# Second norm of an encoder trunk: the second half of the tokens prepared 384 columns at a time, squares on ScalarE summed in a tree

## The chip, the cores and the metric

One core of one Trainium2 chip runs the whole program. The metric is device time in microseconds (us), the median of several runs; lower is better. The engines are named as in the profile: PE (matrix multiplies), DVE (VectorE), ACT (ScalarE), POOL (GpSimd), SP (issues the DMAs).

## The reference

Two layers act on 512 prompt tokens and 256 sample tokens (768 columns here), model width 1024. All is float32.

```
for l in range(DEPTH):                                  # 2
    h = rms_norm(x, norm_mix[l])
    proj = h @ w_in[l]                                  # q, k, v of three mixers
    ...                                                 # global, neighbourhood and dilated attention
    x = x + y @ w_out[l]
    h = rms_norm(x, norm_ffn[l])                        # the part that changes
    gate, up = jnp.split(h @ w_gate_up[l], 2, axis=-1)
    x = x + (jax.nn.silu(gate) * up) @ w_down[l]
```

## The kernel before

**Layout.** Features lie on the 128 partitions (8 chunks `k` of 128), tokens on the columns, and `X` holds the residual. The tokens are three groups `p` of 256; the last norm of a layer takes them in the order 2, 0, 1. For the FFN they are two halves of 384 columns. Every operand of a float32 product is split into a high part (rounded to the matmul's type) and a low part (the rest), and one product is three matmuls (`mm3`, L544: high-high, high-low, low-high).

**Who sets the order.** Each operation is recorded with a priority, a set of engines that it may run on, and a cost. `Plan.emit` simulates the engines with these costs and fixes on which engine, in which buffers and in which order everything is issued. On the chip each engine then runs its list strictly in order, and SP its DMA list too. A cost therefore changes orders and choices, never the work itself, and one changed cost can reorder everything behind it.

**`norm2` (L632)** runs between the attention's output projection (`emit_out`; its last step, L1026, adds into `X`) and the FFN.
- `parts` (L643) makes a high part on ACT (L646) and a low part on DVE (L649, or L652 where a gain is applied as well).
- `half1` splits the first half's columns: operands A and B.
- `half2` does the second half's: C, D and the four sums T1 to T4, built from E1 (L679), T2 (L681), T3 (L684) and T4 (L687). Their scratch buffers lie in the tiles `ppa` (D) and `p`, `bt` (E1, T2, T3, T4). It is called twice, for columns 0 to 128 once groups 2 and 0 are ready, for 128 to 384 once group 1 is.
- `squares` (L586) then squares the group's `X`: 4 squares (L591 on DVE, L592 on ACT), each added (L594) into one of two buffers of the tile `tbm`, folded (L707), split (L560, L561), summed over partitions by two matmuls (`root`, L566), and turned by ACT's Ln and Exp (L569, L571) into `row`, the 1/rms of each token. Since there is one such pair of buffers, the groups take turns.

**`emit_ffn` (L1077)** computes the first two blocks of 128 FFN features (f = 0, 1) as plain products: 192 matmuls of 384 columns in 8 PSUM banks, with weights prepared by `plain` (L1033; low part L1037). DVE multiplies each bank by `row` (L1099), ACT applies SiLU (L1082, after a table load), POOL multiplies gate and up (L1083), and SP writes the result to DRAM (`spill`, L1084). The other 20 blocks use seven products (`PRODUCTS`, L1062) in place of eight, on summed weights (`sums`, L1041: DMA loads L1049, sums L1053, high parts L1056, low parts L1057) and on A, B, D, T1 to T4. The first product of a block is A11 with A.

Of the kernel before, what the change touches and what calls it, by code (L numbers as in the profile page):

```python
# [10 lines left out]
AF = mybir.ActivationFunctionType  # L11
# [35 lines left out]
     nsq='ACT', nadd='DVE', nhi='ACT DVE', nlo='POOL', yhl='DVE POOL', tout=0, tdn=1, n1=2, nf=86, sf=5, om=1,  # L47
     nsq0='ACT DVE', nadd0='DVE POOL', nhi0='ACT DVE', nlo0='POOL,DVE', nsq2='ACT,DVE', nadd2='DVE,POOL', nhi2='ACT',
     nlo2='DVE POOL', qs=0.0, nsp=0.0, nsp2=0.0, w0i=(0, 0, 1, 1), w0d='DVE,POOL', w0p=-19.5, l2=(0, 1), lo=0, vhi='ACT',
# [31 lines left out]
class Plan:  # L81
# [3 lines left out]
    HOP = 0.15  # L85
    FIFO = {"S", "P", "PT", "PTS", "PO", "OT", "OV", "Y", "TB", "BT", "GP", "GS", "W", "RAW", "ACT", "SG", "SQ", "YR", "YT", "RB", "MC", "CS", "QKG", "WG", "WF", "WU", "U", "UL", "UG", "UC", "ROW", "R0", "R1", "RX", "NR", "ND1", "ND2", "H", "H1"}
    GROUP = {"MC": "TB", "WG": "W", "WF": "W", "WU": "W", "UL": "U", "UG": "U", "R0": "RAW", "R1": "RAW", "RX": "RAW", "H1": "H"}
    PSUM = {"D", "S", "PT", "PO", "M", "ANY", "LB"}
# [218 lines left out]
def trunk(ctx: ExitStack, tc: tile.TileContext, t):  # L307
# [324 lines left out]
    def norm2(l, bs):  # L632
# [26 lines left out]

        def half2(ps, a, z, pr):  # L660

            n = z - a
            x = lambda half, kk: X[:, kk, half * HALF + a:half * HALF + z]
            rx = lambda k: [("x", p, kk // 2) for p in ps for kk in (k, k + 4)] + ["gcol"]
            Ds = [P.buf("ND1" if n == 128 else "ND2") for k in range(4)]
            v = lambda b: b[0][:, :n]
            for k in range(4):
                u, D = U[k], Ds[k]
                g0, g1 = gcol[:, l, 2, k:k + 1], gcol[:, l, 2, k + 4:k + 5]
                parts(lambda k=k: x(1, k), u["C"], a, z, g0, rx(k), pr)  # L670
                dve(n, lambda D=D, k=k, g1=g1: DVE.tensor_scalar(v(D), x(1, k + 4), g1, None, op0=OP.mult), r=rx(k), w=[D],
                    prio=pr, fast=True, lock=True, ptr=True)
                parts(lambda D=D: v(D), u["D"], a, z, None, [D], pr)
            pr = L + 198.2
            for k in range(4):
                u, D = U[k], Ds[k]
                g0, g1 = gcol[:, l, 2, k:k + 1], gcol[:, l, 2, k + 4:k + 5]
                E1, T2, T3, T4 = (P.buf("NR") for _ in range(4))
                ew(n, lambda E, E1=E1, k=k: E.tensor_tensor(v(E1), x(1, k), x(0, k), op=OP.subtract), r=rx(k), w=[E1], prio=pr,  # L679
                   on="DVE POOL")  # L680
                dve(n, lambda T2=T2, E1=E1, D=D, g0=g0: DVE.scalar_tensor_tensor(  # L681
                    v(T2), v(E1), g0, v(D), op0=OP.mult, op1=OP.subtract), r=[D, E1, "gcol"], w=[T2], prio=pr, lock=True, ptr=True)
# [45 lines left out]
    def emit_qkv(l, g, bs, wp, gains, rope):  # L728
# [6 lines left out]
        for p in order(g):  # L735
# [91 lines left out]
    def emit_attn(l, g, gs, bs, mc):  # L827
# [15 lines left out]
        for p in order(g):  # L843
# [467 lines left out]
```

## Time and profile before

| what | value |
|---|---|
| median of 3 runs | 1782.69 us (1782.56 to 1784.72) |
| the profiled execution's own time | 1784.08 us |
| its span, first to last instruction | 1782.3 us |
| mean granted PE clock | 0.989 |
| busy: PE, DVE, ACT, POOL | 1712.3, 1310.0, 917.7, 542.0 us |

A busy share is an average over stages with different limits. What matters here is where PE stands still, and what the trace names as the end of the wait (in brackets behind a row of the timeline: idle us, then the releaser). Matmuls are pipelined: the time from one start to the next is a matmul's price, not its duration.

### The profile page before, as it was taken

How to read it: one execution, taken by the hardware profiler on the slowest of the kernel's cores; microseconds unless marked ns; L12 is line 12 of the kernel's file. 1: busy time of each engine (PE TensorE's matmuls, PEld its weight loads, DVE VectorE, ACT ScalarE, POOL GpSimd, SP SyncE). 2: the span in 40 equal slices, each digit the busy share in tenths (PEclk: the TensorE clock that was granted, in tenths of full speed). 3: DMA queues.
4: the chain of work that ended last, by engine and by line, in shares of the span. 5: the costliest groups of instructions: out<-in, count | busy, mean ns of one | idle time of the engine just before them, and what ended most of it. 6: DMA issues, size and time to landing. Idle time of an engine off the chain costs nothing.

```text
span 1782.3 us, 30961 instructions
## 1 busy us (share of the span) xinstructions
PE 1712.3 (96%) x11504; PEld 1682.5 (94%) x11504; DVE 1310.0 (74%) x2511; ACT 917.7 (51%) x2151; POOL 542.0 (30%) x577
## 2 busy tenths in 40 slices
PE   5999999897999999999999999998979999999999
PEld 5999999797999999999999999997979999999999
DVE  7788678699988887543668886777998888864433
ACT  5887577565444444321358775866644444442220
POOL 1565144223233333100015543642223333320000
PEclk9999999998999999999999999999989999999999
DMA  5321111102333332533222201111133333343332
GB/s 158 81 63 49 36 34 51 36 19 91 112 106 103 102 104 90 153 122 104 72 62 62 75 25 36 47 33 36 33 117 100 101 105 104 103 118 123 116 110 72
DMA packets 96200, 145.29 MB, mean 82 GB/s; under 512 B 28720, under 2 KB 58416, under 8 KB 96048
## 3 DMA queue, kind: packets, MB, share of 16 engines
q1 hardware_dynamic: 96048, 143.31, 26.7%
q8 instruction: 90, 1.47, 0.4%
q14 instruction: 62, 0.51, 0.1%
HBM read 122.82 MB, written 20.45 MB: 80 GB/s over the span
## 4 chain that ended last, share of the span: by engine, by line
PE 81%; DVE 10%; ACT 7%; issue 1%; DMA 1%; SPq 0%; DVEq 0%
PE ps L546 24%; PE ps L547 24%; PE ps L548 24%; PE ps L956 3%; PE ps L934 2%; PE ps L875 2%; ACT p L922 1%; ACT u L941 1%; DVE u L652 1%; ACT w L521 1%; DVE w L522 1%; PE ps L807 1%; DVE u L649 1%; DVE x L1026 1%; DVE u L942 1%
## 5 line engine op out<-in xcount | busy, mean ns | idle before, releaser
L548 PE MATMUL ps<-u,w 128*128 128x384 f32 (+1 forms) x1684 | 559.7, 332 | 9.7 <-DVE w L1057 9.7
L546 PE MATMUL ps<-u,w 128*128 128x384 f32 (+1 forms) x1684 | 559.8, 332 | 5.4 <-ACT w L1056 4.6
L547 PE MATMUL ps<-u,w 128*128 128x384 f32 (+1 forms) x1684 | 559.3, 332 | 0.0
L548 PEld LDWEIGHTS ps<-u,w 128*128 128x128 f32 x1684 | 317.8, 189 | 10.6 <-DVE w L1057 10.6
L546 PEld LDWEIGHTS ps<-u,w 128*128 128x128 f32 x1684 | 317.7, 189 | 6.5 <-ACT w L1056 4.9
L547 PEld LDWEIGHTS ps<-u,w 128*128 128x128 f32 x1684 | 317.8, 189 | 0.0
L546 PE MATMUL ps<-w,u 128*128 128x256 f32 x768 | 228.8, 298 | 12.5 <-ACT w L521 9.3
L547 PE MATMUL ps<-w,u 128*128 128x256 f32 x768 | 219.1, 285 | 5.3 <-DVE w L522 5.3
L548 PE MATMUL ps<-w,u 128*128 128x256 f32 x768 | 219.2, 285 | 0.0
L521 ACT CAST w<-raw 128x1024 fp32r<-128x1024 f32 (+2 forms) x102 | 94.9, 932 | 209.2 <-PE ps L547 187.8
L1159 DVE TENSOR_TENSOR x<-x,ps 128x384 f32<-128x384 f32 x96 | 51.4, 553 | 154.4 <-PE ps L548 154.4
L546 PEld LDWEIGHTS ps<-w,u 128*128 128x128 f32 x768 | 148.6, 193 | 14.6 <-ACT w L521 9.3
L547 PEld LDWEIGHTS ps<-w,u 128*128 128x128 f32 x768 | 148.9, 194 | 6.3 <-DVE w L522 5.6
L548 PEld LDWEIGHTS ps<-w,u 128*128 128x128 f32 x768 | 148.5, 193 | 0.0
L546 PE MATMUL ps<-yt,w 128*128 128x256 f32 x392 | 114.3, 291 | 3.9 <-DVE x L1026 3.8
L522 DVE TENSOR_TENSOR w<-raw,w 128x768 fp32r<-128x768 f32 (+2 forms) x87 | 97.2, 1119 | 24.8 <-ACT w L521 17.8
L956 PE MATMUL ps<-u 128*128 128x256 f32 (+1 forms) x592 | 105.6, 296 | 9.4 <-DVE u L942 4.6
L547 PE MATMUL ps<-yt,w 128*128 128x256 f32 x392 | 111.9, 286 | 0.2 <-DVE yt L1012 0.2
L548 PE MATMUL ps<-yt,w 128*128 128x256 f32 x392 | 111.6, 285 | 0.0
L942 DVE TENSOR_TENSOR u<-ps,u 128x512 fp32r<-128x512 f32 (+1 forms) x160 | 97.2, 625 | 18.2 <-ACT u L941 17.4
L875 PE MATMUL ps<-u 128*128 128x256 f32 (+1 forms) x384 | 94.8, 349 | 7.8 <-DVE sm L919 3.9
L956 PEld LDWEIGHTS ps<-u 128*128 128x128 f32 x592 | 84.7, 194 | 14.6 <-DVE u L942 7.1
(253 smaller groups left out, 3711.8 us busy)
## 6 DMA issues: line engine op xcount, KB each, us to landing
raw<-in_w_down SPq DMA_DIRECT2D x48, 384.0 KB, 3.2
raw<-in_w_gu SPq DMA_DIRECT2D x68, 256.0 KB, 3.0
spill<-y SPq DMA_DIRECT2D x86, 192.0 KB, 3.0
raw<-in_w_in SPq DMA_DIRECT2D x32, 512.0 KB, 3.6
p<-in_w_gu SPq DMA_DIRECT2D x51, 256.0 KB, 3.3
ppa<-in_w_gu SPq DMA_DIRECT2D x35, 256.0 KB, 3.2
raw<-in_w_out SPq DMA_DIRECT2D x16, 512.0 KB, 3.6
tbm<-in_w_gu SPq DMA_DIRECT2D x22, 256.0 KB, 2.9
```

The lines of the kernel that those rows point to most:

```text
L521: act(n, lambda hs=hs: ACT.copy(self.flat(0)[:, hs], raw[0][:, hs]), r=[raw], w=[(b, 0) + z], prio=prio)
L522: ew(n, lambda E, hs=hs: E.tensor_tensor(self.flat(1)[:, hs], raw[0][:, hs], self.flat(0)[:, hs].bitcast(F32), op=OP.subtract), r=[raw, (b ...
L546: PE.matmul(out, a[0], b[0], start=start, stop=False, skip_group_check=on)
L547: PE.matmul(out, a[0], b[1], start=False, stop=False, skip_group_check=on)
L548: PE.matmul(out, a[1], b[0], start=False, stop=stop, skip_group_check=on)
L649: ew(n, lambda E: E.tensor_tensor(lo(b, a, z), src(), hi(b, a, z).bitcast(F32), op=OP.subtract), r=r + [(b, 0, a)], w=[(b, 1, a)], prio=pr ...
L652: dve(n, lambda: DVE.scalar_tensor_tensor(lo(b, a, z), src(), g, hi(b, a, z).bitcast(F32), op0=OP.mult, op1=OP.subtract), r=r + [(b, 0, a) ...
L875: PE.matmul(S[0][:, :nk], q, kk[:, k0:k0 + nk], start=i == 0, stop=i == 1)
L934: PE.transpose(pt[0][:, i * 128:(i + 1) * 128], PP[j][0][:, c * 128:(c + 1) * 128], ident)
L942: dve(n, lambda n=n, pt=pt, ps_=ps_: DVE.tensor_tensor(ps_[1][:, :n], pt[0][:, :n], ps_[0][:, :n].bitcast(F32), op=OP.subtract), r=[pt, (p ...
L956: PE.matmul(po[0][:, o:o + wd], v, ps_[i][:, z * wd:(z + 1) * wd], start=first and z == 0 and i == 0, stop=end and (last or more), **({} i ...
L1159: dve(HALF, lambda xv=xv, acc=accs[h]: DVE.tensor_tensor(xv(), xv(), acc[0][:, :HALF], op=OP.add), r=[accs[h]], w=[("x", p, c // 2) for p ...
```

## The change

- `half2` runs once, for all 384 columns of the second half, when group 1 is ready. D's product may run on ACT too (`ndd`).
- The squares of a group go to four buffers of the tile `p` (`HS`), all on ACT (before: ACT and DVE by turns); the adds form a tree and all run on DVE (before, in layer 0, DVE and POOL by turns).
- The squares and the root get a priority of 0.3 behind the group's splits; the sums T1 to T4 keep 198.2. The scratch of E1, T2, T3, T4 is now 5 buffers in `p` and one in `bt`, so that most of it is free only when the last squares are used up.
- The planner's costs for copies of 64 partitions are raised: `kcp1`, `kcp2` (L822) and L966 from 256 to 400 columns, the add L971 from 256 to 336.

```diff
-     nsq0='ACT DVE', nadd0='DVE POOL', nhi0='ACT DVE', nlo0='POOL,DVE', nsq2='ACT,DVE', nadd2='DVE,POOL', nhi2='ACT',
+     nsq0='ACT DVE', nadd0='DVE POOL', nhi0='ACT DVE', nlo0='POOL,DVE', nsq2='ACT', ndd='DVE ACT', nadd2='DVE', nhi2='ACT',
...
-    P.storage("ND1", [(a,) for a in cut(ppa, "ppa", 4, 128)])
-    P.storage("ND2", [(a,) for a in cut(ppa, "ppa", 4, 256, 512)])
-    P.storage("NR", [(a,) for a in cut(pt_, "p", 8, 256) + cut(btr, "bt", 2, 256)])
+    P.storage("ND", [(a,) for a in cut(ppa, "ppa", 4, HALF)])
+    P.storage("NR", [(a,) for a in cut(pt_, "p", 5, HALF) + cut(btr, "bt", 1, HALF)])
...
-    P.storage("H", [tbh])
+    P.storage("HS", [tuple(ptile)])
...
-                dve(n, lambda D=D, k=k, g1=g1: DVE.tensor_scalar(v(D), x(1, k + 4), g1, None, op0=OP.mult), r=rx(k), w=[D],
-                    prio=pr, fast=True, lock=True, ptr=True)
+                ew(n, lambda E, D=D, k=k, g1=g1: E.tensor_scalar(v(D), x(1, k + 4), g1, None, op0=OP.mult), r=rx(k), w=[D],
+                   prio=pr, fast=True, ptr=True, extra=1, on="ndd",
+                   act=lambda D=D, k=k, g1=g1: ACT.activation(v(D), x(1, k + 4), AF.Copy, scale=g1))
...
-            pr, h = bs[p], P.buf("H")
+            pr, h = bs[p], P.buf("HS")
             if p == 2:
                 half1(2, 0, 256, pr)
             elif p == 0:
                 half1(0, 256, HALF, pr)
-                half2((2, 0), 0, 128, pr)
             else:
-                half2((2, 0, 1), 128, HALF, pr)
-            pr += K["nsp2"]
-            squares(p, h, "2", pr)
+                half2((2, 0, 1), pr)
+            pr += 0.3
+            for c in range(4):
+                xc = lambda p=p, c=c: xT(p)[:, 2 * c:2 * c + 2]
+                v = lambda h=h, c=c: h[c].rearrange("p (k t) -> p k t", k=2)
+                ew(512, lambda E, v=v, xc=xc: E.tensor_tensor(v(), xc(), xc(), op=OP.mult), r=[("x", p, c)], w=[(h, c)],
+                   prio=pr, on="nsq2", act=lambda v=v, xc=xc: ACT.activation(v(), xc(), AF.Square))
+            for i, j in ((0, 1), (2, 3), (0, 2)):
+                ew(512, lambda E, h=h, i=i, j=j: E.tensor_tensor(h[i], h[i], h[j], op=OP.add), r=[(h, j)], w=[(h, i)], prio=pr,
+                   on="nadd2")
...
-                ew(256, lambda E, dst=dst, sp=sp: E.tensor_copy(dst(), sp()), r=[pk], w=[(gs[p], "k", p, i)], prio=pr,
+                ew(400 if i else 256, lambda E, dst=dst, sp=sp: E.tensor_copy(dst(), sp()), r=[pk], w=[(gs[p], "k", p, i)], prio=pr,
```

In the changed file the lines behind `norm2` stand 6 further down (L1049 is L1055, L1057 is L1063), those of `mm3`, `root` and `parts` one further up (L566 is L565), and T2, T3, T4 keep theirs. The tree's adds are L707 there, the fold is L713.

DVE in layer 0 at the last group's root, before: the fifth of the eight banks' multiplies (L1099), the root's low part (L561), the other multiplies, then the first sums (L1053) and low parts (L1057) of block f = 2's weights.

```order
L1099 TENSOR_TENSOR y<-ps_77,row 128x384
L561 TENSOR_TENSOR yt<-tbm,yt 128x256
L1099 TENSOR_TENSOR sq<-ps_75,row 128x384
L1099 TENSOR_TENSOR sq<-ps_71,row 128x384
L1099 TENSOR_TENSOR y<-ps_72,row 128x384
L1099 TENSOR_TENSOR y<-ps_74,row 128x384
L1053 TENSOR_TENSOR ppa<-raw 128x512
L1057 TENSOR_TENSOR w<-raw,w 128x512
```

The same root in the changed program: its tree (L707), fold (L713) and low part (L560), among bank multiplies (L1105) and plain weights' low parts (L1043), and behind it the first T2, T3, T4 (L681, L684, L687).

```order
L707 TENSOR_TENSOR p<-p 128x512
L1105 TENSOR_TENSOR y<-ps_73,row 128x384
L707 TENSOR_TENSOR p<-p 128x512
L1043 TENSOR_TENSOR w<-raw,w 128x512
L707 TENSOR_TENSOR p<-p 128x512
L1043 TENSOR_TENSOR w<-raw,w 128x512
L713 TENSOR_TENSOR p<-p 128x256
L1105 TENSOR_TENSOR y<-ps_74,row 128x384
L1105 TENSOR_TENSOR y<-ps_75,row 128x384
L560 TENSOR_TENSOR yt<-p,yt 128x256
L681 SCALAR_TENSOR_TENSOR p<-bt,gcol,ppa 128x384
L684 SCALAR_TENSOR_TENSOR p<-x,gcol,ppa 128x384
```

Some 30 rows further on, still DVE of the changed program, the end of the sums: the last chunk's low parts (L648, L651), the last two bank multiplies, then the first weight sum (L1059) and the low part of A11 (L1063, out of `tbm`).

```order
L648 TENSOR_TENSOR u<-bt,u 128x384
L648 TENSOR_TENSOR u<-p,u 128x384
L651 SCALAR_TENSOR_TENSOR u<-p,gcol,u 128x384
L1105 TENSOR_TENSOR y<-ps_72,row 128x384
L1105 TENSOR_TENSOR y<-ps_73,row 128x384
L1059 TENSOR_TENSOR raw<-tbm 128x512
L1063 TENSOR_TENSOR w<-tbm,w 128x512
```

What moved: before, the last root stood behind all sums and just ahead of the weights; now it stands ahead of all sums, and the low part of the first weight behind all of them. Layer 1 has the same rows in the changed program.

SP in layer 0, before, from the eight loads of the plain weights (L1035) on: three loads of block f = 2 (L1049), a spill (L1084), the fourth load.

```order
L1035 DMA raw<-in_w_gu 128x512 x8
L1049 DMA raw<-in_w_gu 128x512 x3
L1084 DMA spill<-y 128x384
L1049 DMA raw<-in_w_gu 128x512
L1084 DMA spill<-y 128x384
```

SP at the same place in the changed program (L1041, L1055, L1090).

```order
L1041 DMA raw<-in_w_gu 128x512 x8
L1055 DMA tbm<-in_w_gu 128x512 x2
L1055 DMA raw<-in_w_gu 128x512 x2
L1090 DMA spill<-y 128x384 x2
L1090 DMA spill<-sq 128x384
```

All four loads now stand ahead of the first spill, two of them in `tbm`, which the squares no longer use.

## Rows read from the trace of the kernel before

**Rows 1.** The page: PE's busy time and share.

```profile
PE 1712.3 (96%) x11504; PEld 1682.5 (94%) x11504; DVE 1310.0 (74%) x2511; ACT 917.7 (51%) x2151; POOL 542.0 (30%) x577
```

**Rows 2.** Who PE waited for, whole span: total us, times, longest.

```profile
PE ps L548 <- DVE w L1057: 9.7, 2, 9.4
```

**Rows 3.** Busy us of each engine (instructions) in stretches; PEclk, DMA share, GB/s.

```profile
40.00:382.00 342.00, 328.70 (x2628) 316.13 (x2627) 261.51 (x613) 241.69 (x655) 153.05 (x195) 1.00 0.16 46
410.50:420.50 10.00, 1.56 (x5) 0.65 (x3) 7.35 (x18) 6.86 (x14) 1.76 (x3) 0.63 0.00 0
420.50:427.00 6.50, 6.11 (x18) 5.60 (x19) 6.34 (x7) 2.69 (x6) 3.61 (x3) 0.51 0.66 214
433.00:860.00 427.00, 427.00 (x2464) 426.79 (x2463) 300.63 (x454) 162.68 (x298) 104.64 (x82) 1.00 0.36 108
860.00:1262.00 402.00, 386.54 (x3077) 372.94 (x3076) 307.75 (x696) 268.75 (x711) 155.57 (x195) 0.99 0.17 47
1293.00:1303.00 10.00, 0.62 (x4) 0.30 (x3) 10.00 (x24) 3.81 (x10) 1.10 (x1) 0.71 0.41 135
1303.00:1307.50 4.50, 4.50 (x14) 4.50 (x15) 4.46 (x8) 3.84 (x7) 0.00 (x0) 0.50 0.40 121
```

**Rows 4.** Timeline of PE, layer 0: start, us, instruction, [idle before <-releaser].

```profile
410.56 0.34 PE L548 MATMUL ps<-u,w 128*128 128x384 f32 x1
413.90 0.58 PE L566 MATMUL ps<-yt,ones 128*128 128x256 f32 x1 [3.00 <-ACT yt L560]
...
420.54 0.69 PE L546 MATMUL ps<-u,w 128*128 128x384 f32 x1 [4.59 <-ACT w L1056]
...
421.90 0.69 PE L548 MATMUL ps<-u,w 128*128 128x384 f32 x1 [0.36 <-DVE w L1057]
```

**Rows 5.** Timeline of PE, layer 1.

```profile
1293.17 0.34 PE L547 MATMUL ps<-u,w 128*128 128x384 f32 x1
1302.89 0.69 PE L548 MATMUL ps<-u,w 128*128 128x384 f32 x1 [9.38 <-DVE w L1057]
```

**Rows 6.** Timeline of DVE, layer 0.

```profile
363.82 2.45 DVE L652 SCALAR_TENSOR_TENSOR u<-x,gcol,u 128x256 fp32r<-128x256 f32 x6
...
368.60 1.12 DVE L652 SCALAR_TENSOR_TENSOR u<-x,gcol,u 128x128 fp32r<-128x128 f32 x4
...
380.67 1.27 DVE L1026 TENSOR_TENSOR x<-ps,x 128x512 f32<-128x512 f32 x2
...
384.17 0.34 DVE L671 TENSOR_SCALAR ppa<-x,gcol 128x256 f32<-128x256 f32 x1
...
388.25 1.88 DVE L1037 TENSOR_TENSOR w<-raw,w 128x512 fp32r<-128x512 f32 x3
...
405.83 1.47 DVE L1099 TENSOR_TENSOR y<-ps,row 128x384 f32<-128x384 f32 x3
```

**Rows 7.** Timeline of DVE, layer 1.

```profile
1261.49 0.68 DVE L1026 TENSOR_TENSOR x<-ps,x 128x512 f32<-128x512 f32 x1
...
1285.61 1.51 DVE L652 SCALAR_TENSOR_TENSOR u<-p,gcol,u 128x256 fp32r<-128x256 f32 x1
...
1302.16 0.68 DVE L1057 TENSOR_TENSOR w<-raw,w 128x512 fp32r<-128x512 f32 x1
```

**Rows 8.** Timeline of POOL, layer 1.

```profile
1285.34 1.50 POOL L1057 TENSOR_TENSOR w<-raw,w 128x512 fp32r<-128x512 f32 x1 [5.32 <-ACT w L1056]
```

**Rows 9.** Timeline of ACT, layer 0.

```profile
381.29 1.30 ACT L646 ACTIVATE u<-x,gcol 128x256 fp32r<-128x256 f32 x3
...
402.64 0.63 ACT L592 ACTIVATE tbm<-x 128x512 f32<-128x512 f32 x1
...
416.92 1.28 ACT L1082 ACT_TABLE_LOAD   x1
```

**Rows 10.** Groups by line and form: busy us, mean ns of one, idle before.

```profile
L971 DVE TENSOR_TENSOR y<-ps,y 64x256 f32<-64x256 f32 x96 | 39.9, 415 | 12.0 <-ACT y L966 9.6 <-issue 0.3
L822 ACT CAST u<-ps 64x256 fp32r<-64x256 f32 x96 | 35.2, 367 | 10.9 <-DVE u L821 7.4 <-PE ps L811 2.2
```

More of the change, by code (lines that the diff above doesn't have):

```diff
@@ L56 @@
      nadd='DVE POOL', nhi='ACT DVE', nlo='POOL', yhl='DVE POOL', tout=0, tdn=1, n1=2, nf=86, sf=5, om=1,
-     nsq0='ACT', nadd0='DVE POOL', nhi0='ACT', nlo0='POOL', nsq2='ACT,DVE', nadd2='DVE', nhi2='ACT', nlo2='DVE POOL', qs=0.0,
+     nsq0='ACT', nadd0='DVE POOL', nhi0='ACT', nlo0='POOL', nsq2='ACT', ndd='DVE ACT', nadd2='DVE', nhi2='ACT', nlo2='DVE POOL', qs=0.0,
      nsp=0.0, nsp2=0.0, w0i=(0, 1, 2, 2), w0d='DVE,POOL', w0p=-19.5, l2=(0, 1), lo=0, vhi='ACT', vlo='DVE POOL', gu2='POOL',
@@ L85 @@
     HOP = 0.15
-    FIFO = {"S", "P", "PT", "PTS", "PO", "OT", "OV", "Y", "TB", "BT", "GP", "GS", "W", "RAW", "ACT", "SG", "SQ", "YR", "YT", "RB", "MC", "CS", "QKG", "WG", "WF", "WU", "U", "UL", "UG", "UC", "ROW", "R0", "R1", "RX", "NR", "ND1", "ND2", "H", "H1"}
-    GROUP = {"MC": "TB", "WG": "W", "WF": "W", "WU": "W", "UL": "U", "UG": "U", "R0": "RAW", "R1": "RAW", "RX": "RAW", "H1": "H"}
+    FIFO = {"S", "P", "PT", "PTS", "PO", "OT", "OV", "Y", "TB", "BT", "GP", "GS", "W", "RAW", "ACT", "SG", "SQ", "YR", "YT", "RB", "MC", "CS", "QKG", "WG", "WF", "WU", "U", "UL", "UG", "UC", "ROW", "R0", "R1", "RX", "NR", "ND", "HS", "H", "H1"}
+    GROUP = {"MC": "TB", "WG": "W", "WF": "W", "WU": "W", "UL": "U", "UG": "U", "R0": "RAW", "R1": "RAW", "RX": "RAW", "H1": "H", "HS": "H"}
     PSUM = {"D", "S", "PT", "PO", "M", "ANY", "LB"}
@@ L658, in half1, with half2 @@
                 parts(lambda k=k: X[:, k, a:z], b, a, z, gcol[:, l, 2, k:k + 1], [("x", p, k // 2), "gcol"], pr)
-        def half2(ps, a, z, pr):
-            n = z - a
-            x = lambda half, kk: X[:, kk, half * HALF + a:half * HALF + z]
+        def half2(ps, pr):
+            n = HALF
+            x = lambda half, kk: X[:, kk, half * HALF:half * HALF + HALF]
             rx = lambda k: [("x", p, kk // 2) for p in ps for kk in (k, k + 4)] + ["gcol"]
-            Ds = [P.buf("ND1" if n == 128 else "ND2") for k in range(4)]
+            Ds = [P.buf("ND") for k in range(4)]
             v = lambda b: b[0][:, :n]
@@ L669, in half2 @@
                 g0, g1 = gcol[:, l, 2, k:k + 1], gcol[:, l, 2, k + 4:k + 5]
-                parts(lambda k=k: x(1, k), u["C"], a, z, g0, rx(k), pr)
-                dve(n, lambda D=D, k=k, g1=g1: DVE.tensor_scalar(v(D), x(1, k + 4), g1, None, op0=OP.mult), r=rx(k), w=[D],
-                    prio=pr, fast=True, lock=True, ptr=True)
-                parts(lambda D=D: v(D), u["D"], a, z, None, [D], pr)
+                parts(lambda k=k: x(1, k), u["C"], 0, n, g0, rx(k), pr)
+                ew(n, lambda E, D=D, k=k, g1=g1: E.tensor_scalar(v(D), x(1, k + 4), g1, None, op0=OP.mult), r=rx(k), w=[D],
+                   prio=pr, fast=True, ptr=True, extra=1, on="ndd",
+                   act=lambda D=D, k=k, g1=g1: ACT.activation(v(D), x(1, k + 4), AF.Copy, scale=g1))
+                parts(lambda D=D: v(D), u["D"], 0, n, None, [D], pr)
             pr = L + 198.2
@@ L682, in half2 @@
                     v(T2), v(E1), g0, v(D), op0=OP.mult, op1=OP.subtract), r=[D, E1, "gcol"], w=[T2], prio=pr, lock=True, ptr=True)
-                parts(lambda T2=T2: v(T2), u["T2"], a, z, None, [T2], pr)
+                parts(lambda T2=T2: v(T2), u["T2"], 0, n, None, [T2], pr)
                 dve(n, lambda T3=T3, D=D, k=k, g0=g0: DVE.scalar_tensor_tensor(
                     v(T3), x(1, k), g0, v(D), op0=OP.mult, op1=OP.subtract), r=rx(k) + [D], w=[T3], prio=pr, lock=True, ptr=True)
-                parts(lambda T3=T3: v(T3), u["T3"], a, z, None, [T3], pr)
+                parts(lambda T3=T3: v(T3), u["T3"], 0, n, None, [T3], pr)
                 dve(n, lambda T4=T4, T2=T2, k=k, g1=g1: DVE.scalar_tensor_tensor(
                     v(T4), x(0, k + 4), g1, v(T2), op0=OP.mult, op1=OP.add), r=rx(k) + [T2], w=[T4], prio=pr, lock=True, ptr=True)
-                parts(lambda T4=T4: v(T4), u["T4"], a, z, None, [T4], pr)
-                parts(lambda E1=E1: v(E1), u["T1"], a, z, g0, [E1, "gcol"], pr)
+                parts(lambda T4=T4: v(T4), u["T4"], 0, n, None, [T4], pr)
+                parts(lambda E1=E1: v(E1), u["T1"], 0, n, g0, [E1, "gcol"], pr)
         for p in order(NG - 1):
-            pr, h = bs[p], P.buf("H")
+            pr, h = bs[p], P.buf("HS")
             if p == 2:
@@ L965, in emit_attn @@
                 ts = slice(h * 256, h * 256 + 256)
-                act(256, lambda yr=yr, po=po, hs=hs, ts=ts: ACT.copy(yr[0][hs, :], po[0][64:128, ts]), r=[po], w=[(yr, h)],
+                act(400, lambda yr=yr, po=po, hs=hs, ts=ts: ACT.copy(yr[0][hs, :], po[0][64:128, ts]), r=[po], w=[(yr, h)],
                     prio=pr, sbuf=False)
@@ L970, in emit_attn @@
                 ts = slice(h * 256, h * 256 + 256)
-                dve(256, lambda yr=yr, po=po, hs=hs, ts=ts: DVE.tensor_tensor(
+                dve(336, lambda yr=yr, po=po, hs=hs, ts=ts: DVE.tensor_tensor(
                     yr[0][hs, :], po[0][0:64, ts], yr[0][hs, :], op=OP.add), r=[po], w=[(yr, h)], prio=pr)
```

## The prediction

> **What bounds the kernel now.** I read the page first: PE is busy for 96% of the span [rows 1]. That says little, since matmuls overlap: one of 384 columns lasts 0.34 us [rows 4], but in the FFN's long stretch 2464 of them take 427.0 us, 0.173 us each, with no idle time and clock 1.00 [rows 3]. Nothing is to be had there, so I went on to the other stretches of that table. PE is bare at two places, 410.5 to 420.5 (1.56 us busy) and 1293 to 1303 (0.62 us) [rows 3], the end of `norm2` in each layer. The two attention stretches, 342 and 402 us, leave PE idle for 13.3 and 15.5 us, 28.8 together [rows 3].
>
> The list of waits names DVE's low part of a weight (L1057) as the longest [rows 2], and the timelines tell what is late. Layer 0: the 192 plain products are issued by 410.56, the last root waits for its split until 413.90, and the first matmul of block f = 2 starts at 420.54 only, behind ACT's high part, which is queued behind the table load and the SiLUs that need the root (the load stands at 416.92 [rows 9]). Its third matmul, which needs the weight's low part, starts at 421.90 [rows 4]. Layer 1: PE stops after the second matmul of that block at 1293.17 and goes on at 1302.89, when DVE has done the low part at 1302.16 [rows 5, 7]; DVE is busy for all 10.00 us between [rows 3]. So from the last add into `X` (end 381.94 in layer 0, 1262.17 in layer 1 [rows 6, 7]) to that low part DVE needs 40.0 and 40.7 us, and PE has only about 29 to 31 us of other work. Behind each wait the clock is at its lower level, 1.2 of 2.4 GHz: 0.51 and 0.50 of full speed for 6.5 and 4.5 us [rows 3].
>
> **The change part by part.** I price DVE's new list from the last add into `X`, time T, to A11's low part. The order gives the counts.
>
> Prices. L652 on 256 columns: six in 2.45, 0.41 each; on 128: four in 1.12, 0.28 each [rows 6]; the step of 0.13 gives an estimated 0.54 at 384. A two-tensor operation on 384 columns: L1099, three in 1.47, 0.49. On 512: L1037, three in 1.88, 0.63. D's product: 0.34 at 256 columns [rows 6]; I keep 0.34, since the step to 384 matters little for three of them.
>
> *Up to the root.* 3 D products (1.0), 4 low parts of C (2.2), 4 of D (2.0), 4 low parts of plain weights and 3 tree adds (7 x 0.63 = 4.4), 3 bank multiplies (1.5), fold and root's low part (0.8): 11.8. ACT in that time has 4 C parts, 4 D casts, one D product, Ln and Exp, 4 squares and 3 weight casts; with 0.43 for a scaled part of 256 columns and 0.63 for a square [rows 9], 0.5 a piece elsewhere and 0.6 for a weight cast, that is about 10. It is close behind DVE, so DVE will wait for a square once or twice: I add 1.0 (0 to 2).
>
> *The sums.* 16 operations at 0.54 (8.6), 12 low parts, 3 E1 and 5 bank multiplies at 0.49 (9.8), one weight sum and the low part itself (1.3): 19.7. As a check from the other side: merging the widths saves 0.41 + 0.28 - 0.54 = 0.15 on each of the 20 scaled operations, 3.0 a layer, and six squares that leave DVE save 6 x 0.63 = 3.8; 6.8 in all, which is what layer 1 gains by the sum (40.7 - 34.0). In layer 0 six adds come back from POOL, three of 512 columns and three of 256, at most 3 us; with them go POOL's delays.
>
> *POOL beside DVE.* In layer 1 an L652 that usually takes 0.41 took 1.51: it began at 1285.61 while POOL ran from 1285.34 to 1286.84 [rows 7, 8]. In the new order POOL has four gate products (L1089) behind its first E1, some beside the sums: 0 to 4 such delays of 1.1, 0 to 4.4. I take 1.5, since most of the gate products wait for late bank multiplies.
>
> Sum: 11.8 + 1.0 + 19.7 + 1.5 = **34.0 us**, against 40.0 and 40.7. T itself moves: 30 plain matmuls stand ahead of the last output projection where 24 stood, 6 x 0.173 = 1.0 later. The third matmul of block 2 then starts near 381.94 + 1.0 + 34.0 = 416.9 in layer 0, 5.0 ahead of 421.90, and near 1297.2 in layer 1, 5.7 ahead of 1302.89. PE still stops, for 4 to 6 us a layer, so I keep the stretch at the low clock as it is.
>
> What else must be in time: the four weight loads now stand ahead of the spills and two go to `tbm`, so data and ACT's cast are there before DVE. The sums cannot start before the last root (their scratch lies in `p`), which costs nothing if DVE has other work; until then it has the 11.8 us. T2 is needed 24 matmuls (4.2 us) behind A11's start, and it is complete before A11's low part. The steps behind (S1, S2 and their low parts, 5 x 0.63 = 3.2) fit under those 24 matmuls. Squares and D's product on ACT cost PE nothing while ACT stays under DVE's 34 us.
>
> The raised costs: a copy of 64 x 256 takes 0.367 on ACT, the add 0.415 on DVE [rows 10]; the planner's cost functions gave 0.265 and 0.337 for them (0.052 + 256/1200 and 0.07 + 256/960) and now give 0.385 and 0.42. They add no work, yet the attention of both layers is dealt anew. No row says what the new order costs; the bounds are the 28.8 us that PE idles there now, less or more. I take 0, since the new costs lie nearer the rows, and plus or minus 4 for the likeliest case.
>
> Total: 5.0 + 5.7 = 10.7. The profiled execution took 1784.08 (span 1782.3 and 1.8 around it): 1773.4. The median of the runs lies 1.4 below it, so I forecast **1772 us**. A measurement tells about 0.2% (3.6 us) from no change: faster is below 1779.1, slower above 1786.3.
>
> **The rivals.**
> - *The wait only moves* (1781). If every gate product on POOL holds DVE for its whole length, not one operation in three, the four take 4 x 1.5 = 6.0 in place of 1.5 [rows 8]: the chain is 38.5, the gain 10.7 - 9.0 = 1.7, near 1781. For it: A11's low part, which the list of waits blames, now stands behind all sums. Against it: 24 DVE instructions fit into the 10.00 us of layer 1's wait, with POOL busy for 1.10 of them [rows 3], so most of the sums have POOL's side free.
>  The Trainium skill, "SBUF — State Buffer", section "SBUF: two separate sides", says that a VectorE operation with two SBUF inputs and a GpSimd operation that reads SBUF exclude each other for a whole instruction. By that rule this rival would be the forecast; the 1.51 us agree with it for one instruction, and no row here shows it for all kinds.
> - *The wait vanishes* (1760). If DVE and ACT stay ahead, PE runs through: the third matmul follows two others (0.35 us) on 410.73 in layer 0, 10.8 us earlier, and 0.17 us on 1293.17 in layer 1, 9.5 earlier; the half-speed stretches give back up to half of 6.5 and 4.5 us, of which I count 3. That is 23.3 in all, 1784.1 - 23.3 - 1.4 = 1759.4. Against it: the sum would have to be wrong by 6 us a layer.
> - *Slower: the new order of the attention* (1787 and up). PE loses there what norm2 gains as soon as its 28.8 us of idle time grow by 10.7, and it is measurably slower from 14.3 on, half as much again. For it: every queue is in-order and the order differs from early in layer 0. Against it: the planner's new costs are the measured ones within 5%, and PE there is 96% busy whatever the order has been.
>
> **How the numbers follow.** Forecast (1766 to 1778): 0.60. Wait moves: 0.13. Wait vanishes: 0.12. Attention: 0.15. Faster 0.60 + 0.12 = 0.72, same 0.13, slower 0.15. The range 1762 to 1784 takes in the moved wait and half of the vanished one; about 0.06 lies below it and 0.13 above.
>
> **What would show it.** Right: in both layers PE's last root (L565) stands amid the plain products with a wait under 1.5 us; PE then stops once, for 4 to 6 us, on DVE's L1063; from the last add into `X` to the end of that low part there are 34 us, of them some 13 to the root's split. The load of the fourth weight is issued ahead of any spill. Wrong: a wait of PE at that place for ACT or a DMA, DVE idle among the sums for want of scratch buffers or casts (a chain near 40), or idle time of PE in the attention stretches that differs from 13.3 and 15.5 us by more than 4.

## The result, and the profile after

| | median | runs |
|---|---|---|
| before | 1782.67 us | 1782.56 to 1784.72 |
| changed | 1761.39 us | 1760.31 to 1764.65 |

The ratio is 0.9881 (95% interval 0.9864 to 0.9898): 21.3 us faster. The forecast was 1772 us, 10.7 faster, in a range of 1762 to 1784. The direction was right; the gain was twice as large, and the time fell 0.6 us below the range.

The page of the changed kernel, its row of busy times (answers to [rows 1]), and from the list of PE's waits the entry that answers to [rows 2]:

```profile
PE 1703.2 (97%) x11504; PEld 1678.5 (95%) x11504; DVE 1295.1 (74%) x2430; ACT 917.0 (52%) x2117; POOL 532.7 (30%) x556
```

```profile
PE ps L547 <- DVE w L1063: 8.2, 2, 4.1
```

The number of matmuls is the same; DVE has 81 instructions fewer. The wait for A11's low part is now PE's only one at this place, 4.1 us in each layer. PE's timeline at it, layer 0 and layer 1 (answers to [rows 4, 5]):

```profile
390.39 0.40 PE L565 MATMUL ps<-yt,ones 128*128 128x256 f32 x2
...
406.40 0.34 PE L546 MATMUL ps<-u,w 128*128 128x384 f32 x1
410.83 0.44 PE L547 MATMUL ps<-u,w 128*128 128x384 f32 x1 [4.10 <-DVE w L1063]
...
1272.45 0.34 PE L546 MATMUL ps<-u,w 128*128 128x384 f32 x1
1276.91 0.69 PE L547 MATMUL ps<-u,w 128*128 128x384 f32 x1 [4.12 <-DVE w L1063]
```

The last root (first row) is now summed amid the plain products, without a wait; before it came 23.5 us later, after a wait of 3.00 [rows 4]. DVE's timeline, layer 0 and then layer 1 (answers to [rows 6, 7]), shows the last add into `X`, the root's low part, and A11's low part:

```profile
377.92 0.68 DVE L1032 TENSOR_TENSOR x<-ps,x 128x512 f32<-128x512 f32 x1
...
389.44 0.42 DVE L560 TENSOR_TENSOR yt<-p,yt 128x256 fp32r<-128x256 f32 x1
...
410.10 0.68 DVE L1063 TENSOR_TENSOR w<-tbm,w 128x512 fp32r<-128x512 f32 x1
...
1243.98 0.69 DVE L1032 TENSOR_TENSOR x<-ps,x 128x512 f32<-128x512 f32 x1
...
1276.17 0.69 DVE L1063 TENSOR_TENSOR w<-tbm,w 128x512 fp32r<-128x512 f32 x1
```

From the end of the last add (378.60, 1244.67) to that of the low part (410.78, 1276.86) DVE needs 32.2 us in both layers, where it needed 39.9 and 40.7 (the prediction's 40.0 runs to PE's start at 421.90 [rows 4]). And the last add itself comes earlier: 3.3 us in layer 0 (381.94 before).

The table of stretches (answers to [rows 3]). The second attention stretch begins at the same distance ahead of the FFN's last add as 860 did before:

```profile
40.00:378.60 338.60, 325.91 (x2638) 315.68 (x2637) 260.72 (x603) 243.50 (x654) 150.52 (x190) 1.00 0.17 48
406.50:410.50 4.00, 0.24 (x2) 0.00 (x0) 4.00 (x9) 1.79 (x4) 0.75 (x1) 1.00 0.85 278
410.50:416.00 5.50, 5.17 (x20) 5.17 (x21) 5.47 (x9) 2.56 (x5) 2.96 (x1) 0.69 0.33 93
847.00:1244.70 397.70, 385.42 (x3086) 373.30 (x3085) 307.74 (x689) 270.27 (x708) 151.87 (x186) 1.00 0.17 49
1272.00:1277.00 5.00, 0.88 (x6) 0.56 (x4) 5.00 (x11) 2.07 (x4) 1.17 (x1) 0.79 0.71 231
1277.00:1284.00 7.00, 7.00 (x28) 7.00 (x29) 6.66 (x10) 4.06 (x8) 2.53 (x1) 0.66 0.41 132
```

The two attention stretches take 338.6 + 397.7 = 736.3 us in place of 342 + 402 = 744 [rows 3]. That is a third of the whole gain, in a part of the kernel to which the change adds no work and from which it takes none. (Six more plain matmuls even stand ahead of the last output projection now, 30 where 24 stood.) While PE waits, DVE is busy for all 4.00 and 5.00 us: the end of `norm2` is still DVE's. The granted clock behind the wait is 0.69 and 0.66, part of the stretch at the lower of its two levels, 1.2 GHz.

In terms of the span: 1782.3 - 1758.5 = 23.8 us, of which 7.9 is the earlier last add (3.3 in layer 0, 4.6 in layer 1, counted from layer 0's last FFN add on), 16.2 the shorter chains from the last add to A11's low part (7.7 and 8.5), and -0.3 what follows (1.9 gained in layer 0, 2.2 lost in layer 1).

### The profile page after: what moved, and what is told of

It reads as the page before. It is cut to its first block, busy times and chain, and to the rows that moved or that the text cites. A ratio compares the mean times of both kernels' runs of the same rounds, so it can differ in the third digit from the quotient of the medians.

```text
span 1758.5 us, 30838 instructions
## 1 busy us (share of the span) xinstructions
PE 1703.2 (97%) x11504; PEld 1678.5 (95%) x11504; DVE 1295.1 (74%) x2430; ACT 917.0 (52%) x2117; POOL 532.7 (30%) x556
## 5 line engine op out<-in xcount | busy, mean ns | idle before, releaser
L962 PE MATMUL ps<-u 128*128 128x256 f32 (+1 forms) x592 | 102.2, 292 | 6.0 <-DVE y L977 3.6
L521 DVE TENSOR_TENSOR w<-raw,w 128x768 fp32r<-128x768 f32 (+2 forms) x84 | 88.9, 1060 | 17.5 <-ACT w L520 12.0
L881 PE MATMUL ps<-u 128*128 128x256 f32 (+1 forms) x384 | 93.4, 350 | 5.0 <-DVE sm L925 2.7
L962 PEld LDWEIGHTS ps<-u 128*128 128x128 f32 x592 | 82.7, 191 | 10.7 <-DVE y L977 4.6
```

What stands on the lines that cost most here:

```text
L521: ew(n, lambda E, hs=hs: E.tensor_tensor(self.flat(1)[:, hs], raw[0][:, hs], self.flat(0)[:, hs].bitcast(F32), op=OP.subtract), r=[raw, (b ...
L881: PE.matmul(S[0][:, :nk], q, kk[:, k0:k0 + nk], start=i == 0, stop=i == 1)
L962: PE.matmul(po[0][:, o:o + wd], v, ps_[i][:, z * wd:(z + 1) * wd], start=first and z == 0 and i == 0, stop=end and (last or more), **({} i ...
```

## The experiments

Each time stands beside runs of the kernel before on the same chip, whose medians were 1782.5 (E1 to E4), 1783.5 (E5 to E8), 1783.2 (E9 to E12), 1782.7 (E13 to E16) and 1782.6 us (E17, E18). The theory after the result: the planner's three numbers dealt attention anew and gave the part that the forecast took as zero. The rival: the new norm itself frees the attention's tail.

### E1 and E2: the two parts of the change apart

E1 is the kernel before with the three numbers; E2 is the changed kernel without them.

```diff
-                ew(256, lambda E, dst=dst, sp=sp: E.tensor_copy(dst(), sp()), r=[pk], w=[(gs[p], "k", p, i)], prio=pr,
+                ew(400 if i else 256, lambda E, dst=dst, sp=sp: E.tensor_copy(dst(), sp()), r=[pk], w=[(gs[p], "k", p, i)], prio=pr,
...
-                act(256, lambda yr=yr, po=po, hs=hs, ts=ts: ACT.copy(yr[0][hs, :], po[0][64:128, ts]), r=[po], w=[(yr, h)],
+                act(400, lambda yr=yr, po=po, hs=hs, ts=ts: ACT.copy(yr[0][hs, :], po[0][64:128, ts]), r=[po], w=[(yr, h)],
...
-                dve(256, lambda yr=yr, po=po, hs=hs, ts=ts: DVE.tensor_tensor(
+                dve(336, lambda yr=yr, po=po, hs=hs, ts=ts: DVE.tensor_tensor(
```

> The kernel before with nothing changed but the three numbers that the planner is given for the last two key copies (400 for 256), the copy of the attention product's second half (400) and the addition of the out-projection's inputs (336); second half of the tokens, its sums and its squares stay as they were. Theory A (the new order of attention is where the unforeseen gain comes from): about 8 to 10 us faster, some 1773 us, with the last addition into X at about 379 to 380 us in layer 0 (381.94 before). Rival B (the attention's tail is freed by the rewritten norm, and the numbers are worth nothing): within 3 us of 1782.7, last addition still at about 382 us.

> The changed kernel with the three numbers put back to 256, so that only the norm before the feed-forward part is changed. Theory A: what the forecast took for that part, 11 to 16 us, so 1767 to 1772 us, with the last addition into X at 381.9 to 383 us in layer 0. Rival B: nothing is lost by putting the numbers back, 1760 to 1763 us, last addition at about 379 us.

E1: 1774.44 us, ratio 0.9958 (0.9946 to 0.9971), 8.1 us faster. E2: 1768.47, ratio 0.9921 (0.9909 to 0.9934), 14.0 faster. Their sum is 22.1, the change's gain 21.3. The attention stretches of E1 and then of E2, and between them the last adds of E1 and E2 in layer 0:

```profile
40.00:377.80 337.80, 325.09 (x2634) 314.86 (x2633) 261.04 (x608) 241.29 (x654) 153.95 (x195) 1.00 0.17 47
857.30:1253.20 395.90, 382.33 (x3076) 370.24 (x3075) 307.72 (x696) 267.38 (x707) 153.13 (x189) 1.00 0.17 48
```

```profile
376.36 1.41 DVE L1026 TENSOR_TENSOR x<-ps,x 128x512 f32<-128x512 f32 x2
```

```profile
380.54 1.28 DVE L1032 TENSOR_TENSOR x<-ps,x 128x512 f32<-128x512 f32 x2
```

```profile
40.00:381.90 341.90, 328.61 (x2628) 316.02 (x2627) 259.13 (x602) 243.21 (x653) 149.79 (x190) 1.00 0.17 48
851.30:1252.70 401.40, 386.03 (x3080) 372.12 (x3079) 306.48 (x683) 270.18 (x708) 154.04 (x192) 1.00 0.17 48
```

With the numbers the two stretches sum to 733.7 us, without them to 743.3, nearly the 744 of before. The rival falls: the new norm leaves the attention as long as it was.

The numbers do not act on the attention alone. In E1, with the old norm, the chain from the last add to A11's low part takes 41.5 and 41.6 us where it took 39.9 and 40.7, so part of the 10.3 us by which the stretches shrank is lost again. In E2, with the new norm in the old order, the chain is 34.6 and 34.5 us, some 2.4 longer than in the change (last adds until 381.82 and 1252.69). E2's low parts of A11 in layer 0 and layer 1:

```profile
415.71 0.68 DVE L1063 TENSOR_TENSOR yt<-raw,yt 128x512 fp32r<-128x512 f32 x1
...
1286.53 0.68 DVE L1063 TENSOR_TENSOR yt<-raw,yt 128x512 fp32r<-128x512 f32 x1
```

### E3 and E5: wide sums or new squares alone

Both have the three numbers. E3 is the changed kernel with the squares of before:

```diff
-    P.storage("HS", [tuple(ptile)])
+    P.storage("HS", [tbh])
...
-            pr += 0.3
-            for c in range(4):
...
-            for i, j in ((0, 1), (2, 3), (0, 2)):
...
+            squares(p, h, "2", pr)
```

> The changed kernel with the three new numbers and the sums formed 384 columns wide, but the squares of the second norm as before (two tiles of 256 columns for each part, dealt to ScalarE and VectorE, added by VectorE or GpSimd, not held back). My working of the forecast put about half of the chain's gain on the way from the last addition to the root (14.5 us before, 11.8 after) and the other half on the sums. Theory A: 3 to 8 us slower than the changed kernel, 1764 to 1769 us. Rival: the squares cost nothing on this way because the root is not what PE waits for, 1760 to 1763 us.

E5 is the other half: E1 with the squares and adds of the change, and `half2` still called twice, for 128 and 256 columns.

```diff
-            pr += K["nsp2"]
-            squares(p, h, "2", pr)
+            pr += 0.3
+            for c in range(4):
...
+            for i, j in ((0, 1), (2, 3), (0, 2)):
...
```

> The kernel before with the three numbers for the planner (400, 400, 336) and with the new squares alone: all on ScalarE, added in a tree on VectorE in the four tiles of p, 0.3 behind the parts; the second half of the tokens and its sums stay in two pieces of 128 and 256 columns. E3 was the other half of it, the merged sums without the new squares, and gained nothing over E1 (1774.07 against 1774.44). Theory R (the root ahead of the sums carries the gain; merging saves DVE at most 3.0 us a layer): 1761 to 1768 us, with the last root's split on DVE about 12 us behind the last addition into X. Rival (neither half is worth anything alone, as DVE's list only becomes short enough with both): 1771 to 1775 us.

E3: 1774.07 us, ratio 0.9956 (0.9944 to 0.9969). E5: 1773.95, ratio 0.9942 (0.993 to 0.9955). Against E1's 1774.44 either half alone gives nothing that can be told from noise (the intervals of E1, E3 and E5 overlap), and both together give 13 us. Both expectations that I favoured were missed. In E3, PE and ACT in layer 0:

```profile
410.94 0.39 PE L565 MATMUL ps<-yt,ones 128*128 128x256 f32 x1 [1.02 <-ACT yt L559]
...
416.61 0.69 PE L545 MATMUL ps<-u,w 128*128 128x384 f32 x1 [4.59 <-ACT w L1054]
```

```profile
412.99 1.28 ACT L1080 ACT_TABLE_LOAD   x1
...
415.95 0.60 ACT L1054 CAST w<-raw 128x512 fp32r<-128x512 f32 x1
```

The last root is still late, so the first sum-block's weight is cast on ACT behind Ln, Exp, the table load and four SiLUs, as before: a chain through the root. In E5 the root is early and another chain ends last. PE, then DVE:

```profile
391.46 0.40 PE L566 MATMUL ps<-yt,ones 128*128 128x256 f32 x2
...
411.28 0.34 PE L548 MATMUL ps<-u,yt 128*128 128x384 f32 x1
421.29 0.69 PE L546 MATMUL ps<-u,w 128*128 128x384 f32 x1 [9.67 <-ACT w L1063]
```

```profile
418.50 0.41 DVE L649 TENSOR_TENSOR u<-p,u 128x256 fp32r<-128x256 f32 x1
...
419.91 0.68 DVE L1060 TENSOR_TENSOR raw<-tbm 128x512 f32<-128x512 f32 x1
```

PE's 9.67 us wait names ACT's cast (of S2, the block's third matrix), but ACT waited for the weight sum at 419.91, and that stands on DVE behind the last of the T sums at 418.50. So the stretch from the root to the end of the sums is what counts; in E5, and below it in the changed kernel:

```profile
391.10:418.85 27.75, 20.52 (x119) 20.20 (x118) 26.79 (x69) 15.94 (x41) 7.00 (x6) 0.92 0.10 33
```

```profile
389.90:408.60 18.70, 16.84 (x98) 16.52 (x96) 18.43 (x35) 12.20 (x24) 3.75 (x3) 1.00 0.16 51
```

It is 69 DVE instructions against 35 and 27.75 us against 18.70, beside 7.00 against 3.75 us of POOL. There are two chains of nearly equal length into PE's stop at this place, and the change cuts both: with one half alone the other chain still ends as late. The traces show these two waits; that each half is worth exactly nothing is not shown, since another order by itself moves the time by some us (last experiment).

### E4 and E8: the parts of the first weights ahead of the sums

E4 gives the high and low parts of A11 and A12 in block f = 2 a priority just ahead of the T sums; E8 treats S2 and the additions that form it likewise.

```diff
-            act(width, lambda m=m: ACT.copy(hi(m), raw(m)), r=[q[m]], w=[(b[m], 0)], prio=prio)
+            pm = early if early is not None and m in ("A11", "A12") else prio
+            act(width, lambda m=m: ACT.copy(hi(m), raw(m)), r=[q[m]], w=[(b[m], 0)], prio=pm)
...
-            wb = sums([t["w_gu"][l, f, i] for i in range(4)], 512, pr - 1.5, ends)
+            wb = sums([t["w_gu"][l, f, i] for i in range(4)], 512, pr - 1.5, ends, base - 1.9 if f == FIRST_F else None)
```

> The changed kernel with the high and low parts of the first two matrices of the first block of sums put ahead of the later sums in the order, as soon as these matrices are formed. PE stops once in each layer for 4.1 us on the low part (from 406.40 to 410.56 us in layer 0), and its clock falls there. Theory: that wait goes, and with it the half-clock stretch behind it: 4 to 8 us faster, 1753 to 1757 us. Rival: the wait moves to the next matrix's parts, which now come later by two additions and two copies: within 2 us of 1761.4.

> E4 (first two matrices' parts of the first block of sums put ahead, 1759.1 us) with the third matrix treated likewise: the three additions that form it, its high and its low part stand ahead of the later sums too. In E4 PE stopped 3.8 us in each layer for that matrix's high part. Theory: the wait goes, since the sums need only be complete two products later, and with it the half-clock stretch: 1752 to 1757 us. Rival: DVE's whole list is the bound, so the same wait appears at the sums' parts instead: 1758 to 1761 us.

E4: 1759.09 us, ratio 0.9871 (0.9856 to 0.9886). E8: 1759.04, ratio 0.9861 (0.9847 to 0.9874). E16 is the changed kernel once more: 1760.56 us, 0.9875 (0.9861 to 0.989). The intervals overlap, so a gain isn't shown. PE in E4 and in E8, layer 0:

```profile
413.44 0.69 PE L545 MATMUL ps<-u,yt 128*128 128x384 f32 x1 [3.76 <-ACT yt L1063]
```

```profile
414.40 0.44 PE L545 MATMUL ps<-u,yt 128*128 128x384 f32 x1 [2.96 <-ACT y L1122]
```

The wait goes from A11 to S2, 2.6 us later, and then to a PSUM bank that ACT has not yet emptied. Each time it shrinks a little, 4.10, 3.76, 2.96 us. In E8 that ACT copy stands in ACT's list behind its casts of the last T sums, which wait for DVE. So DVE's list is what PE waits for, whichever entry stands last.

> The changed kernel itself beside the others of this call, since E4 and E8 lie only 2.3 us below the 1761.4 us that it took in another: 1760 to 1763 us. If it comes out at 1759 or less, E4 and E8 gained nothing.

### E6, E7 and E9 to E14: which numbers, and how exact

All are the kernel before with other numbers for the key copies, the product's copy on ACT, and the add on DVE (256, 256, 256 before).

| run | numbers | median, us | ratio (95% interval) |
|---|---|---|---|
| E1 | 400, 400, 336 | 1774.44 | 0.9958 (0.9946 to 0.9971) |
| E6 | 400, 256, 256 | 1777.67 | 0.9968 (0.9956 to 0.9981) |
| E7 | 256, 400, 336 | 1786.73 | 1.0014 (1.0005 to 1.0023) |
| E13 | 400, 400, 256 | 1779.88 | 0.9983 (0.9974 to 0.9992) |
| E14 | 400, 256, 336 | 1784.71 | 1.0005 (0.9995 to 1.0014) |
| E9 | 384, 384, 320 | 1773.72 | 0.9944 (0.9928 to 0.9961) |
| E10 | 404, 404, 340 | 1775.27 | 0.9954 (0.9939 to 0.9969) |
| E11 | 328, 328, 296 | 1774.93 | 0.9954 (0.9939 to 0.9969) |
| E12 | 560, 560, 430 | 1781.23 | 0.9989 (0.9979 to 0.9998) |

> The kernel before with one number changed: the last two key copies are planned as 400 in place of 256. Theory Y (what counts is the attention product's copy and addition, since PE waited for that addition at the end of the last group in both layers): within 3 us of 1782.5 and the last addition into X at about 382 us in layer 0. Rival K (the key copies, at the head of each group, carry it): 1773 to 1777 us, last addition at about 378 us.

> The kernel before with two numbers changed: the copy of the attention product's second half is planned as 400 and the addition as 336, both in place of 256; key copies as before. Theory Y: 1773 to 1777 us, last addition into X at about 378 us in layer 0, no wait of PE over 2 us for that addition near 350 us. Rival K: within 3 us of 1782.5. A third outcome, a time that doesn't fit the sum with E6 (together they gave 8.1 us), would speak for an order that is found by luck rather than by truer numbers.

> The kernel before with the planner's three numbers at 384, 384 and 320, 4 to 5% below those of the change (400, 400, 336, which gave 1774.4 us). Theory T (truer numbers make a better order): within 1.5 us of 1774.4. Theory L (any other number draws another order of some thousand rows, and its time is luck): anywhere from 1770 to 1788, more than 3 us from 1774.4 in this run or in the next.

> The kernel before with the planner's three numbers at 404, 404 and 340, 1% above those of the change. Theory T: within 1.5 us of 1774.4. Theory L: anywhere from 1770 to 1788, more than 3 us from 1774.4 in this run or in the last.

> The kernel before with half of the change's steps in the planner's three numbers: 328, 328 and 296. Theory T: between before and the change, 1776 to 1781 us. Theory L: no relation to the step; outside 1774 to 1783, or to be told from the others only by chance.

> The kernel before with the steps doubled: 560, 560 and 430, far above what the trace shows for these instructions. Theory T: worse than E1, 1777 us or more, as the numbers are wrong again on the other side. Theory L: as likely to be faster than 1774 as slower.

> The kernel before with the key copies and ScalarE's copy of the attention product planned as 400, VectorE's addition left at 256. Key copies alone gave 5.8 us (E6), copy and addition alone cost 3.2 (E7), all three gave 8.1 (E1). If ScalarE's number is what was wrong (both raised ones are its copies), this gives what E1 gave, 1773 to 1776 us. If the addition is needed as well, 1777 to 1783 us.

> The kernel before with the key copies planned as 400 and VectorE's addition as 336, ScalarE's copy of the attention product left at 256. If ScalarE's number is what was wrong: no better than key copies alone, 1776 to 1781 us. If the addition is what the key copies lacked: 1773 to 1776 us.

Four sets in which all three numbers rise together, by half of the step to just over all of it, lie within 1.6 us of each other. Twice the step loses most of the gain, as Theory T said; half of it loses none, which Theory T did not say. Raising one or two of the three gives anything from 5.8 us faster to 3.2 slower than before, and the effects don't add. The key copies alone (E6) give 5.8 of E1's 8.1 us; with the product's copy added only 2.8 are left, and with the add in its place none (2.0 slower, which its interval does not tell from before). The attention stretches of E7 sum to 746.9 us, those of E1 to 733.7:

```profile
40.00:384.70 344.70, 329.07 (x2640) 317.17 (x2640) 262.98 (x615) 242.24 (x657) 150.45 (x191) 1.00 0.16 46
863.00:1265.20 402.20, 384.27 (x3077) 371.64 (x3076) 306.22 (x686) 267.63 (x707) 159.33 (x199) 1.00 0.16 47
```

But a short attention is not yet a gain. E14's stretches sum to 735.5 us, less than the changed kernel's, and it is no faster than before. Its stretches, and then its low parts of A11 in both layers:

```profile
40.00:373.80 333.80, 323.76 (x2615) 312.61 (x2614) 257.49 (x613) 240.56 (x651) 140.40 (x185) 1.00 0.17 47
858.30:1260.00 401.70, 385.48 (x3070) 372.80 (x3070) 307.43 (x695) 268.07 (x707) 143.85 (x187) 0.99 0.16 47
```

```profile
419.42 1.33 DVE L1057 TENSOR_TENSOR w<-raw,w 128x512 fp32r<-128x512 f32 x1 [1.03 <-ACT w L1056]
...
1303.06 0.68 DVE L1057 TENSOR_TENSOR w<-raw,w 128x512 fp32r<-128x512 f32 x1
```

Its last adds end at 373.78 and 1260.02, and from there to A11's low part it needs 47.0 and 43.7 us, where the kernel before needed 39.9 and 40.7. E9, whose last add in layer 0 ends at 372.10, needs 46.8 there. So what comes early out of the attention is lost at the old norm's list. No single number carries the gain, and nearness to the rows does not tell the time either. Why the planner's orders come out as they do is open.

### E15, E17 and E18: do the gains add up?

E17 is the changed kernel with 384, 384, 320; E15 is E8 with the same numbers; E18 is E8 with 328, 328, 296.

> E8 (three matrices' parts ahead of the later sums, 1759.0 us) with the planner's three numbers at 384, 384 and 320, with which E9 was as fast as E1. If what the norm gives and what the order of the attention gives add up: 1757 to 1760 us. If the two are bound up with each other through the order of the plain products (E9 had the last addition into X at 372 us and yet no better time): 1760 to 1766 us.

> The changed kernel with the planner's three numbers at 384, 384 and 320 and nothing else. E15 had these numbers and three matrices' parts ahead, and took 1754.8 us; E8, with 400, 400 and 336, took 1759.0. If the numbers alone gave E15 its 4 us, this is 1756 to 1758 us. If they need the parts ahead of the sums, 1760 to 1763 us.

> E8 with 328, 328 and 296, which without the rest of the change were as good as the full numbers (E11, 1774.9 against 1774.4 us). If gains add up: 1757 to 1761 us. If each set of numbers draws its own luck with this norm: a scatter of several us, 1752 to 1766.

E15: 1754.77 us, ratio 0.9841 (0.9825 to 0.9858). E17: 1756.35, 0.9854 (0.9839 to 0.9868). E18: 1763.01, 0.9895 (0.9878 to 0.9911). Sets that were equal on the kernel before differ here by 8 us: 1754.8, 1759.0 and 1763.0 for 384, 400 and 328 on one and the same norm. That is the scatter which the order brings by itself. Part of it can be followed: E17's last add in layer 0 ends at 373.46, nearly as early as E9's with the same numbers, but with the new norm its chain takes 34.1 us and not 46.8, so the early add is kept. E15 has the lowest time of all, 28 us below before and 6 below the change.

## Why the prediction was off, step by step

- **"the attention of both layers is dealt anew ... I take 0": wrong, and the step that failed.** The numbers alone are worth 8.1 us (E1), twice the 4 that I allowed. The argument was that they add no work and that "PE there is 96% busy whatever the order". But of the 7.7 us by which the two stretches shrank, idle time gave 3.8 (28.8 [rows 3] to 12.7 + 12.3 = 25.0) and busy time 3.9 (328.70 + 386.54 to 325.91 + 385.42), with 19 matmuls more. Busy time is not a fixed amount of work: a matmul held up for less than its own drawn length still counts as busy. As an estimate from the matmuls' start-to-start times, with each shape at its own low price (0.12 us for 256 columns), such hold-ups fill some 74 us of the two stretches' busy time before and 67 in the change. My bound from idle time saw half of what an order can change, and my sign that this step had failed, idle time off by more than 4, would not have shown it. And "the new costs lie nearer the rows" compares them with drawn lengths: from start to start, ACT's copies of 64 x 256 take 0.27 us in one place and 0.38 in the next (98.34, 98.61 and 98.99 us, before), so neither 0.265 nor 0.385 fits all.
- **"T itself moves ... 1.0 later": charged to the wrong part.** The six more plain matmuls stand ahead of the last output projection in the changed kernel (30), but in E2, with the same norm, 24 as before, and its last add ends at 381.82 in layer 0, before 381.94. They came with the new numbers' order, which brought the last add 3.3 us earlier all the same. With the 2.0 us that I charged for it, the norm's part was forecast as 10.7; E2 gave 14.0.
- **The chain of 34.0 us: right in kind.** It is 32.2 in the changed kernel and 34.6 and 34.5 in E2, so 34.0 lies within what the order moves. In the changed kernel the root's low part ends 11.3 us behind the last add (389.86) where the working had 11.8 + 1.0: the wait for ACT did not come. From there to A11's low part it is 20.9 (to 410.78) against 19.7 + 1.5. In sum 16.2 us saved for a forecast 12.7.
- **"I keep the stretch at the low clock as it is": right in the sum only.** Behind A11's low part layer 0 gained 1.9 us in the change (the clock there was 0.69 over 5.5 us, before 0.51 over 6.5 [rows 3]) and 3.2 in E2; layer 1 of the change lost 2.2, for a cause that was not looked for.
- **"0.15 on each of the 20 scaled operations, 3.0 a layer": right as the price of the merge alone.** E5 shows the sums' stretch 9.05 us longer without it, and its trace divides them, as an estimate: about 3 for the widths (a scaled operation takes 0.26 + 0.40 us in two pieces and 0.53 in one, start to start), 3.3 for delays beside POOL (4.7 against 1.4), 2 for two bank multiplies and two weight sums more in the stretch, 0.7 for waits. E3 shows that the merge buys nothing until the root is early. The other half of that check was too high: of the "six squares that leave DVE" only four stood behind the last add in either layer, so that its 6.8 met 40.7 - 34.0 was partly luck.
- **"PE still stops, for 4 to 6 us a layer": right**, 4.1, once in each layer, on L1063. The root without a wait, the loads ahead of the spills and a granted clock that falls behind the wait are all there.
- **The rivals.** "The wait only moves" is wrong for the change, but E4 and E8 show it for the next step. "The wait vanishes" named 1760 us, which is nearly what came, by another way: the wait is still there. "Slower: the new order of the attention" had the right place and the wrong sign, and E7 shows that this sign was possible: 1786.7 us with two of the three numbers.
- **POOL beside DVE: right.** I took 1.5 us a layer; in layer 0 of the changed kernel three DVE instructions are held, by 0.53, 0.12 and 0.75 us, 1.4 in sum. The rule of the Trainium skill that I set beside it ("SBUF — State Buffer", section "SBUF: two separate sides"), whole-instruction exclusion, agrees with the changed kernel's trace (last section). It did not bring the rival's 6.0 us: only three gate products stood beside the sums, and beside one of them DVE had bank multiplies out of PSUM (403.23), which were not held.

## What to carry to other kernels

Where a planner deals the order from costs, a changed cost is a change of the whole program, and it has to be forecast with a scatter (here some 8 us, 0.5%) and measured apart from the edit that it comes with. Idle time of an engine that is "96% busy" is no upper bound for what another order gives: compare the time for the same instructions, and then look whether the next wait lets the gain through (E14). And before pricing a chain, look for the second one that ends at the same wait: two halves that each gain nothing can gain 13 us together.

## What was not expected of the hardware

In these traces a DVE operation that read two tensors from SBUF and started while a POOL instruction ran ended about 0.41 us behind POOL's end (at 384 columns). The changed kernel, layer 0, POOL's gate product:

```profile
404.44 1.33 POOL L1089 TENSOR_TENSOR sq<-sq 128x384 f32<-128x384 f32 x1
```

and DVE beside it:

```profile
404.82 1.36 DVE L684 SCALAR_TENSOR_TENSOR bt<-x,gcol,ppa 128x384 f32<-128x384 f32 x1
406.11 0.61 DVE L687 SCALAR_TENSOR_TENSOR p<-x,gcol,p 128x384 f32<-128x384 f32 x1
```

The first took 1.36 in place of 0.61 us and ended at 406.18, 0.41 behind POOL's 405.77. It is not a matter of the scaled form. A plain two-tensor operation in the same kernel, POOL first and then DVE, took 1.37 in place of 0.55 and also ended 0.41 behind POOL:

```profile
1440.54 1.33 POOL L1133 TENSOR_TENSOR sq<-sq,row 128x384 f32<-128x384 f32 x1
```

```profile
1440.91 1.37 DVE L1133 TENSOR_TENSOR sq<-sq,row 128x384 f32<-128x384 f32 x1
```

Where one of the two tensors lay in PSUM, DVE was not held. Three such adds took 0.49 each beside POOL, whose row stands first:

```profile
1424.72 1.30 POOL L1063 TENSOR_TENSOR w<-raw,w 128x512 fp32r<-128x512 f32 x1 [9.25 <-ACT w L1062]
```

```profile
1424.46 1.48 DVE L1126 TENSOR_TENSOR y<-y,ps 128x384 f32<-128x384 f32 x3
```

The changed kernel's trace has 65 operations of 384 columns with two tensors from SBUF that began 0.1 us or more behind the start of a POOL instruction and 0.3 or more ahead of its end: all 65 ended 0.41 to 0.42 us behind it. Of 132 with one tensor from PSUM none was held (0.54 to 0.56 us). In E3 one plain operation seems to be an exception. It began 0.32 us behind a POOL instruction and kept its 0.55, and the scaled one behind it took 1.09. POOL first, then DVE:

```profile
407.65 1.46 POOL L705 TENSOR_TENSOR tbm<-tbm 128x256 f32<-128x256 f32 x1 [7.09 <-DVE tbm L593]
```

```profile
407.97 0.55 DVE L648 TENSOR_TENSOR u<-bt,u 128x384 fp32r<-128x384 f32 x1
408.44 1.09 DVE L687 SCALAR_TENSOR_TENSOR p<-x,gcol,p 128x384 f32<-128x384 f32 x1
```

But that POOL instruction took 1.46 us where the shortest of E3's three on this line took 0.74, so it may itself have been held by DVE first. Spans on POOL are rough, and no run isolated the two.
